# Whole-tile loads of the experts' weights, values transposed one projection later, and the last rows' norm in two halves

## The chip, the core and the metric

The kernel runs as one program on one core of one Trainium2 chip. The core has a matrix engine (PE, with PEld for the loads of its stationary operand), a vector engine (DVE), an activation engine (ACT), GpSimd (POOL), a sync engine (SP) that here only issues transfers, and 16 DMA engines shared by all queues. The metric is the device time of one execution in microseconds (us); a run's time is given, and the median over runs.

## The reference, cut to what matters

The computation takes 512 tokens of width 1024 through two residual blocks. Three of its parts are touched by the change.

```python
# first block: mixture of experts, 64 experts of width 512, two for each token
def expert_block(args):
    xb, e = args
    hid = jax.nn.silu(xb @ w_gate[e]) * (xb @ w_up[e])
    return hid @ w_down[e]
# second block: bidirectional gated linear attention, 4 heads with values of 128
...
contrib = jnp.einsum('bhncd,bhnce->bhnde', k * jnp.exp(b_last - b), v)
...
o = rmsnorm_2(o, norm_g) * jax.nn.silu(r.reshape(B, T, GLA_HEADS, GLA_DV))
# second block: squared-relu MLP of width 4096, then the last norm
h = h + sqrelu_mlp(h, ln_ff_g[l], w_ff1[l], w_ff2[l])
return rmsnorm_2(h, ln_final_g)
```

All is float32. The weights of the experts are 3 x 64 matrices of 2 MiB, together 402 MB, and each is read once.

## The kernel before

**Order in time.** The first block's mixer and the routing run until about 410 us, the experts until about 1360 us, the second block's attention, linear attention and MLP until the end. A framework schedules the instructions of each engine within a stretch by itself; the experts' matmuls are pinned in program order (`mm`, L985), and SP issues its loads in one queue.

**Experts.** `experts` (L963) walks over 32 pairs. For one pair it multiplies the gathered tokens with the gate matrices of both experts (L1059), then with the up matrices, combines the pair before into the residual `H` (`bring`, L1187 and L1190), transposes the hidden rows, and multiplies them with the two down matrices in two passes of 512 columns (names `y` and `tp`). A product walks over k-slices `j` and, inside, over the two experts `s`, whose halves of 64 columns run side by side on PE. So a product needs both experts' tiles from its first step on.

**Their weights.** `ring` (L113) hands out 9 buffers of 2 MiB in turn; a load into a buffer waits until PE has read what the load overwrites, region by region. `load` cuts a matrix into `n` pieces along the k-slices and issues each as one transfer of 128 rows, one row for a partition:

```python
n = 4 if e0 < 12 else 2
one = lambda shape, w, e: [self.ring(shape, w[e + s], 8 if e == 2 and w is wg else n) for s in range(2)]
```

`e0` is the first expert of a pair. A row is therefore 4 KB long for the first twelve experts and 8 KB after that. SP holds at most 8 loads in flight: the ninth waits for the first to land. The last pair comes in interleaved halves and quarters through `pair` (L131), the down matrices of the last two pairs after all gate and up matrices.

**Linear attention.** `values(n)` (L1591) projects one head's values (24 matmuls into `pj`, three for each k-slice: L178 and L179 read `wH`, L180 reads `wL`, the two parts into which `wsplit` cuts the weights on ACT and DVE), scales them on DVE into `x`, and transposes `x` on PE in four pieces (L1597) into `vt`. `decays` fills DVE with exponentials' products, `states` (L1629) builds the running states from `vt` and `kd`, `head` (L1654) projects the gate and makes the output of a head.

**End.** `wout_tail` (L379) multiplies the last part of the MLP for four blocks `t` of 128 rows in two halves of 512 columns and adds each half to `H` (L399). `each(t)` normalizes the block's rows (`normed`, L1319: square with sum on ACT, `rsqrt_of` on one column, one product on DVE) and stores it.

Of the kernel before, what the change touches and what calls it, by code (L numbers as in the profile page):

```python
# [6 lines left out]
FT = mybir.dt.float32  # L7
# [3 lines left out]
AF = mybir.ActivationFunctionType  # L11
OP = mybir.AluOpType
# [3 lines left out]
P = 128  # L16
T = 512
D = 1024
KT = 8
NT = 4  # L20
EPS = 1e-6
# [7 lines left out]
class Net:  # L29
# [346 lines left out]

        return [[t[:, 2 * half:2 * half + 2, :] for t in tiles] for half in range(2)]

    def wout_tail(self, W, h, mix, rs, each, between=None, behind=None):  # L379

        nc = self.nc
        banks = {}

        def product(t, half):
            if half == 0:
                banks[t] = [self.psum(("pj", "tp")[t % 2]) for _ in range(2)]
            for k in range(4):
                w = W[k // 2, half]
                m = self.mm3(banks[t][half], (mix[0][:, k, t * P:(t + 1) * P], mix[1][:, k, t * P:(t + 1) * P]),
                             (w[0][:, k % 2, :], w[1][:, k % 2, :]), k == 0, k == 3)  # L390
                if behind and k == 0:
                    self.order(behind, m)

        def add(t, half):
            o = h[:, t, half * 512:half * 512 + 512]
            if rs is None:
                nc.vector.tensor_tensor(o, banks[t][half], o, OP.add)
            else:
                nc.vector.scalar_tensor_tensor(o, banks[t][half], rs[:, t:t + 1], o, op0=OP.mult, op1=OP.add)  # L399
        product(0, 0)  # L400
        product(0, 1)
        if between:
            between()
        for t in range(NT):
            add(t, 0)
            add(t, 1)
            if t + 1 < NT:
                product(t + 1, 0)
            if each and 1:
                each(t)  # L410
            if t + 1 < NT:
                product(t + 1, 1)
            if each and not 1:
                each(t)
# [548 lines left out]
    def experts(self, keep, pool, front, inner, then):  # L963
        tc, nc, i = self.tc, self.nc, self.ins
        V = nc.vector
# [3 lines left out]
        wd = i["w_down"][0].rearrange("e (p j) n -> e p j n", j=4)  # L969

        def weights(e0):
            n = 4 if e0 < 12 else 2
            one = lambda shape, w, e: [self.ring(shape, w[e + s], 8 if e == 2 and w is wg else n) for s in range(2)]
            up, dn = [P, KT, 512], [P, 4, D]
            if e0 == 60:

                late.extend((lambda: one(dn, wd, 60), lambda: self.pair(dn, (wd[62], wd[63]))))
                return [(one(up, wg, 60), one(up, wu, 60), None),
                        (self.pair(up, (wg[62], wg[63])), self.pair(up, (wu[62], wu[63])), None)]
            return [(one(up, wg, e0), one(up, wu, e0), one(dn, wd, e0))]  # L980
# [62 lines left out]
        halves = [slice(half * 512, half * 512 + 512) for half in range(2)]  # L1043
# [7 lines left out]
        for i in range(32):  # L1051
            q, pr = i // 2, i % 2
            e0 = 2 * i
# [30 lines left out]
            rs, gs, at = vals[q]  # L1084
            r, g = rs[:, pr:pr + 1], gs[:, pr:pr + 1]
# [6 lines left out]
            turn = gained(i + 1) if 0 < i < 31 else iter(())  # L1092
# [3 lines left out]
            p = self.psum("tp")  # L1096
# [72 lines left out]
            if i == 3:  # L1169
                n = self.overflow_count(keep, front.tile([P, 64], FT, name="more", tag="eq", bufs=1))  # L1170
# [390 lines left out]
    def gla(self, small, pool, wp, w_in, A, mix, w_out, gates):  # L1561
        nc, i = self.nc, self.ins
        mm = nc.tensor.matmul
        V = nc.vector
# [7 lines left out]
        for n in range(4):  # L1572
            p = self.proj(self.wsplit(wp, wqk[:, :, n * P:(n + 1) * P], P), A)
# [5 lines left out]
        for tp in range(2):  # L1579
            p = self.psum("tp")  # L1580
            for t in range(2):
                for n in range(2):
                    o = (2 * t + n) * P
                    c = (2 * tp + t) * P
# [4 lines left out]
        vt = one("vt", [P, NT, 512])  # L1589

        def values(n):  # L1591
            p = self.proj(self.wsplit(wp, wv[:, :, n * P:(n + 1) * P], P), A)
            x = tmp("x")
            V.tensor_tensor(x, p, self.rb, OP.mult)
            p = self.psum("tp")
            for c in range(NT):
                nc.tensor.transpose(p[:, c * P:(c + 1) * P], x[:, c * P:(c + 1) * P], self.ident)  # L1597
            self.copy(vt[:, :, n * P:(n + 1) * P], p.rearrange("p (c k) -> p c k", c=NT))

        def decays(pr):  # L1600

# [49 lines left out]

        rs, og = [], []

        def head(hd, qd, ki, st):  # L1654
            s = hd % 2
            p = self.proj(self.wsplit(wp, wr[:, :, hd * P:(hd + 1) * P], P), A)
            sr = tmp("sr")
            V.tensor_tensor(sr, p, self.rb, OP.mult)
            nc.scalar.activation(sr, sr, AF.Silu)
            M = []  # L1660
            for d in range(2):
                p = self.psum("sc")
                for c in range(NT):
                    cs = slice(c * P, (c + 1) * P)
                    mm(p[:, cs], ki[s][half(d), cs], qd[s][half(d), cs], start=True, stop=True)
                t = pool.tile([P, NT, P], FT, name="M", bufs=2)
                V.tensor_tensor(t, p.rearrange("p (c k) -> p c k", c=NT),
                                mask[d][:, None, :].to_broadcast([P, NT, P]), OP.mult)
                M.append(t)
            o = self.psum("y")  # L1670
            for c in range(NT):
                cs = slice(c * P, (c + 1) * P)
                todo = [(vt[:, c, hd * P:(hd + 1) * P], M[d][:, c, :], cs) for d in range(2)]
                for n in (2 * c, 2 * c + 1):
                    ns = half(n)
                    todo.append((st[:, n, :], qd[s][:, ns], ns))
                for x, (a, b, to) in enumerate(todo):
                    last = mm(o[:, to], a, b, start=x == 0, stop=x == len(todo) - 1)  # L1678
            sq = tmp("sq")
            nc.scalar.activation(sq, o, AF.Square)  # L1680
            if s == 0:
                og.append(pool.tile([P, 2, T], FT, name="og", tag="kt" if hd else "la0", bufs=1))
            V.tensor_tensor(og[hd // 2][:, s, :], o, sr, OP.mult)
            p = self.psum("tp")
            for c in range(NT):
                mm(p[:, c:c + 1], sq[:, c * P:(c + 1) * P], self.ones[:, :1], start=True, stop=True)
            rs.append(self.rsqrt(small, p[:, :NT], NT, 1.0 / 128))
            return last
# [12 lines left out]


        *qk0, kd0 = decays(0)
        values(0)
        values(1)
        st = {0: states(0, qk0[2], kd0)}
        values(2)
        st[1] = states(1, qk0[2], kd0)
        *qk1, kd1 = decays(1)
        values(3)  # L1710
        wr = self.ring([P, KT, 512], w_in[:, :, 2560:3072])
        wt = self.ring([P, 4, D], w_out[:, 4:8, :])
        head(0, *qk0[:2], st[0])
        st[2] = states(2, qk1[2], kd1)
        last = head(1, *qk0[:2], st[1])
        normed(0, last)
# [9 lines left out]
    def ffn(self, pool, wp, A, r3):  # L1726
        nc, i, h = self.nc, self.ins, self.H
        V = nc.vector
        w1 = i["w_ff1_2"][0].rearrange("(k p) n -> p k n", p=P)
        w2 = i["w_ff2_2"][0].rearrange("(k p) n -> p k n", p=P)  # L1730
        for q in range(4):
            mixes = []
            for b in range(2):
                w = self.ring([P, KT, 512], w1[:, :, (2 * q + b) * 512:(2 * q + b + 1) * 512])
                m = self.mixtile(pool)
                mixes.append(m)
                for j in range(4):
                    p = self.proj(self.wsplit(wp, w[:, :, j * P:(j + 1) * P], P), A, P, 2 if q + b == 0 and j < 2 else 1)
                    r = pool.tile([P, T], FT, name="r", bufs=2)
                    nc.scalar.activation(r, p, AF.Relu)  # L1740
                    s = pool.tile([P, T], FT, name="s", bufs=2)
                    V.scalar_tensor_tensor(s, p, 0.0, r, op0=OP.max, op1=OP.mult)
                    self.split(m[0][:, j, :], m[1][:, j, :], s)
            w = [self.ring([P, 4, D], w2[:, 8 * q + 4 * b:8 * q + 4 * b + 4, :]) for b in range(2)]
            srcs = lambda half, s: w[s // 2][:, 2 * (s % 2):2 * (s % 2) + 2, half * 512:half * 512 + 512]
            if q < 3:
                self.wout(wp, h, srcs, mixes, r3)
            else:
                self.wout(wp, h, srcs, mixes[:1], r3)
                g = self.row(pool, "ln_final_g_2")  # L1750
                out = self.out[0].rearrange("(c p) d -> p c d", p=P)
                self.wout_tail(self.tail_weights(wp, self.halves(self.mixtile(pool)), w[1]), h, mixes[1], r3,
                               lambda c: nc.sync.dma_start(out[:, c, :], self.normed(pool, h[:, c, :], g)))


class Begin:
# [111 lines left out]
```

## Time and profile before

| | us |
|---|---|
| three runs | 2029.66, 2025.50, 2029.56 |
| median | 2029.56 |
| profiled execution | 2025.04 |
| its span, first to last instruction | 2023.3 |
| PE busy in it | 1928.0 (95%) |
| DVE busy | 946.3 (47%) |
| ACT busy | 534.7 (26%) |
| q1, the loads that SP issues | 483.63 MB, 60% of 16 DMA engines |

Times are read within the span. A row of a timeline gives its start, how long it or its merged group took, the engine, the line of the kernel, the operation with its output and inputs, a count, and in brackets how long the engine stood idle ahead of it and what ended that. A busy PE is not PE at its peak: matmuls are pipelined and a group's time is that of the group.

### The profile page before, as it was taken

The numbers are of one execution on the slowest core, as the hardware profiler recorded it, in microseconds if no ns is written. First come the engines' busy times: TensorE is split into PE (matmuls) and PEld (weight loads), VectorE is DVE, ScalarE is ACT, GpSimd is POOL, SyncE is SP. The second block draws the span as 40 slices with busy tenths as digits, with TensorE's granted clock in tenths as the row PEclk, the third lists the DMA queues.
The fourth block names the chain that finished last, engine by engine and source line by source line (L and its number), as shares of the span: only waits on it lengthen the run. The fifth ranks groups of instructions, "written<-read, shape, count | busy, mean of one in ns | idle before, by whom it ended". The sixth has DMA issues, their size and how long they took to land. (4 is left out here: it accounts for less than half of the span.)

```text
span 2023.3 us, 24002 instructions
## 1 busy us (share of the span) xinstructions
PE 1928.0 (95%) x9535; PEld 1209.0 (60%) x9535; DVE 946.3 (47%) x1891; ACT 534.7 (26%) x900; POOL 191.2 (9%) x245
## 2 busy tenths in 40 slices
PE   7999999999999999999999899999999999999998
PEld 5788777734444344343343344348767788888886
DVE  6764667733543243253243243235656654444355
ACT  5773445311010000000000000024443343223232
POOL 5211333110000000000000000002201010000000
PEclk9999999999999999999999999999999999999999
DMA  7312022799999999999999999984212112313211
GB/s 204 115 43 83 32 81 97 268 343 415 415 425 425 424 424 424 424 424 425 424 423 423 421 424 422 422 335 87 92 42 84 43 52 84 125 48 119 103 64 42
DMA packets 114777, 494.24 MB, mean 244 GB/s; under 512 B 16492, under 2 KB 23091, under 8 KB 74984
## 3 DMA queue, kind: packets, MB, share of 16 engines
q1 hardware_dynamic: 107720, 483.63, 60.0%
q0 software_dynamic: 6352, 6.96, 1.5%
q10 hardware_dynamic: 592, 2.10, 0.3%
q8 instruction: 76, 1.25, 0.3%
q14 instruction: 37, 0.30, 0.0%
HBM read 500.68 MB, written 6.15 MB: 250 GB/s over the span
## 5 line engine op out<-in xcount | busy, mean ns | idle before, releaser
L986 PE MATMUL pj<-w,xg 128*64 128x512 f32 x1696 | 467.8, 603 | 47.1 <-DMA w<-in_w_up 45.8
L986 PEld LDWEIGHTS pj<-w,xg 128*64 128x64 f32 x1696 | 152.5, 139 | 334.0 <-issue 257.5
L159 DVE TENSOR_TENSOR wL<-w,wH 128x1024 fp32r<-128x1024 f32 x135 | 167.4, 1241 | 201.1 <-ACT wH L158 198.4
L158 ACT CAST wH<-w 128x1024 fp32r<-128x1024 f32 x136 | 142.3, 1048 | 336.3 <-PE pj L179 163.9
L1091 DVE SCALAR_TENSOR_TENSOR hid<-pj,slots,hid 128x512 f32<-128x512 f32 x30 | 22.5, 751 | 426.8 <-PE pj L986 412.4
L1190 DVE TENSOR_TENSOR H<-sc,H 128x512 f32<-128x512 f32 x248 | 156.5, 683 | 6.2 <-PE sc L1187 3.5
L986 PE MATMUL pj<-w16x,xg 128*64 128x512 f32 x352 | 153.7, 619 | 0.9 <-DMA w16x<-in_w_gate 0.9
L1187 PE MATMUL sc<-yH,ST 128*128 128x512 f32 x256 | 112.7, 440 | 0.6 <-DVE H L1190 0.6
L843 POOL DMA_INDIRECT rows<-hd,tok x31 | 31.7, 1022 | 817.1 <-DVE gates L837 574.3
L1100 ACT COPY hT<-tp 128x512 f32<-128x512 f32 x32 | 18.8, 587 | 339.9 <-PE tp L1098 339.9
L180 PE MATMUL pj<-n3H,wL 128*128 128x512 f32 (+1 forms) x272 | 103.6, 381 | 0.8 <-DVE wL L159 0.8
L178 PE MATMUL pj<-n3H,wH 128*128 128x512 f32 (+1 forms) x272 | 103.6, 381 | 0.0
L179 PE MATMUL pj<-n3L,wH 128*128 128x512 f32 (+1 forms) x272 | 103.5, 380 | 0.0
L178 PE MATMUL pj<-A,wH 128*128 128x512 f32 x240 | 97.3, 405 | 4.0 <-ACT wH L158 2.8
L1187 PE MATMUL sc<-yL,ST 128*128 128x512 f32 x252 | 99.9, 396 | 0.0
L178 PE MATMUL sc<-wH,mixH 128*128 128x512 f32 x252 | 98.5, 391 | 0.4 <-ACT wH L158 0.4
L179 PE MATMUL sc<-wL,mixH 128*128 128x512 f32 x252 | 98.4, 390 | 0.1
L180 PE MATMUL sc<-wH,mixL 128*128 128x512 f32 x252 | 98.2, 390 | 0.0
L179 PE MATMUL pj<-A,wH 128*128 128x512 f32 x240 | 96.8, 403 | 0.0
L180 PE MATMUL pj<-A,wL 128*128 128x512 f32 x240 | 96.2, 401 | 0.5 <-DVE wL L159 0.5
L986 PE MATMUL y<-w,hT 128*64 128x512 f32 x336 | 78.0, 599 | 0.7 <-DMA w<-in_w_down 0.7
L986 PE MATMUL tp<-w,hT 128*64 128x512 f32 x336 | 76.5, 592 | 0.0
(586 smaller groups left out, 3279.6 us busy)
## 6 DMA issues: line engine op xcount, KB each, us to landing
w<-in_w_up SPq DMA_DIRECT2D x88, 1024.0 KB, 20.8
w<-in_w_gate SPq DMA_DIRECT2D x84, 1024.0 KB, 19.6
w<-in_w_down SPq DMA_DIRECT2D x70, 1024.0 KB, 19.6
w16x<-in_w_down SPq DMA_DIRECT2D x32, 1024.0 KB, 20.2
w<-in_w_ff SPq DMA_DIRECT2D x16, 2048.0 KB, 7.8
w<-in_w_in SPq DMA_DIRECT2D x12, 2048.0 KB, 10.4
w<-in_w_up SPq DMA_DIRECT2D x40, 512.0 KB, 9.9
w16x<-in_w_gate SPq DMA_DIRECT2D x20, 1024.0 KB, 19.8
```

The lines of the kernel that those rows point to most:

```text
L158: a = nc.scalar.copy(H, src)
L159: b = (engine or nc.vector).tensor_tensor(L, src, H.bitcast(FT), OP.subtract)
L178: m = mm(out, lH, rH, start=first, stop=False)
L179: mm(out, lH, rL, start=False, stop=False)
L180: mm(out, lL, rH, start=False, stop=last)
L843: self.nc.gpsimd.indirect_dma_start(out=rows, out_offset=None, in_=self.hd[:, :], in_offset=bass.IndirectOffsetOnAxis(ap=tok, axis=0), bou ...
L986: return self.pin(nc.tensor.matmul(*a, **k))
L1091: V.scalar_tensor_tensor(hid, pu, r, hid, op0=OP.mult, op1=OP.mult)
L1100: nc.scalar.copy(hT.rearrange("p j s -> p (j s)"), p)
L1187: m = nc.tensor.matmul(p, ST[:n, t * P:(t + 1) * P], y[:n], start=k == 0, stop=k == len(mms) - 1)
L1190: nc.vector.tensor_tensor(h[:, t, hs], p, h[:, t, hs], OP.add)
```

## The change

Three edits. The pieces of a weight matrix are fewer: two up to expert 7, one from expert 8 on, the very first gate matrices of expert 2 and 3 and the last pair as before. `values` returns its transposes as a function, and the callers run it after the next projection, the last one inside the first `head`. In `wout_tail` a hook runs after the last block's first half is added: it squares that half and multiplies it with the gain; the rest of the norm then covers the second half alone on DVE, with the first half scaled on ACT and stored through ACT's queue.

```diff
--- before.py
+++ after.py
@@ -376,7 +376,7 @@
 
         return [[t[:, 2 * half:2 * half + 2, :] for t in tiles] for half in range(2)]
 
-    def wout_tail(self, W, h, mix, rs, each, between=None, behind=None):
+    def wout_tail(self, W, h, mix, rs, each, between=None, behind=None, half_done=None):
 
         nc = self.nc
         banks = {}
@@ -403,6 +403,8 @@
             between()
         for t in range(NT):
             add(t, 0)
+            if half_done and t == NT - 1:
+                half_done()
             add(t, 1)
             if t + 1 < NT:
                 product(t + 1, 0)
@@ -969,7 +971,7 @@
         wd = i["w_down"][0].rearrange("e (p j) n -> e p j n", j=4)
 
         def weights(e0):
-            n = 4 if e0 < 12 else 2
+            n = 2 if e0 < 8 else 1
             one = lambda shape, w, e: [self.ring(shape, w[e + s], 8 if e == 2 and w is wg else n) for s in range(2)]
             up, dn = [P, KT, 512], [P, 4, D]
             if e0 == 60:
@@ -1592,10 +1594,13 @@
             p = self.proj(self.wsplit(wp, wv[:, :, n * P:(n + 1) * P], P), A)
             x = tmp("x")
             V.tensor_tensor(x, p, self.rb, OP.mult)
-            p = self.psum("tp")
-            for c in range(NT):
-                nc.tensor.transpose(p[:, c * P:(c + 1) * P], x[:, c * P:(c + 1) * P], self.ident)
-            self.copy(vt[:, :, n * P:(n + 1) * P], p.rearrange("p (c k) -> p c k", c=NT))
+
+            def turn():
+                p = self.psum("tp")
+                for c in range(NT):
+                    nc.tensor.transpose(p[:, c * P:(c + 1) * P], x[:, c * P:(c + 1) * P], self.ident)
+                self.copy(vt[:, :, n * P:(n + 1) * P], p.rearrange("p (c k) -> p c k", c=NT))
+            return turn
 
         def decays(pr):
 
@@ -1651,9 +1656,11 @@
 
         rs, og = [], []
 
-        def head(hd, qd, ki, st):
+        def head(hd, qd, ki, st, between=None):
             s = hd % 2
             p = self.proj(self.wsplit(wp, wr[:, :, hd * P:(hd + 1) * P], P), A)
+            if between:
+                between()
             sr = tmp("sr")
             V.tensor_tensor(sr, p, self.rb, OP.mult)
             nc.scalar.activation(sr, sr, AF.Silu)
@@ -1701,16 +1708,19 @@
 
 
         *qk0, kd0 = decays(0)
-        values(0)
-        values(1)
+        a = values(0)
+        b = values(1)
+        a()
         st = {0: states(0, qk0[2], kd0)}
-        values(2)
+        a = values(2)
+        b()
         st[1] = states(1, qk0[2], kd0)
         *qk1, kd1 = decays(1)
-        values(3)
+        a()
+        a = values(3)
         wr = self.ring([P, KT, 512], w_in[:, :, 2560:3072])
         wt = self.ring([P, 4, D], w_out[:, 4:8, :])
-        head(0, *qk0[:2], st[0])
+        head(0, *qk0[:2], st[0], a)
         st[2] = states(2, qk1[2], kd1)
         last = head(1, *qk0[:2], st[1])
         normed(0, last)
@@ -1749,8 +1759,30 @@
                 self.wout(wp, h, srcs, mixes[:1], r3)
                 g = self.row(pool, "ln_final_g_2")
                 out = self.out[0].rearrange("(c p) d -> p c d", p=P)
-                self.wout_tail(self.tail_weights(wp, self.halves(self.mixtile(pool)), w[1]), h, mixes[1], r3,
-                               lambda c: nc.sync.dma_start(out[:, c, :], self.normed(pool, h[:, c, :], g)))
+                halves = [slice(0, 512), slice(512, D)]
+                x = pool.tile([P, D], FT, name="nl", bufs=1)
+                ss = pool.tile([P, 2], FT, name="nl2", bufs=1)
+
+                def half_done():
+
+                    nc.scalar.activation(x[:, halves[1]], h[:, 3, halves[0]], AF.Square, accum_out=ss[:, 0:1])
+                    V.tensor_tensor(x[:, halves[0]], h[:, 3, halves[0]], g[:, halves[0]], OP.mult)
+                    V.tensor_scalar(ss[:, 0:1], ss[:, 0:1], 1.0 / D, EPS, op0=OP.mult, op1=OP.add)
+
+                def tile_done(c):
+                    if c < 3:
+                        nc.sync.dma_start(out[:, c, :], self.normed(pool, h[:, c, :], g))
+                        return
+                    nc.scalar.activation(x[:, halves[1]], h[:, 3, halves[1]], AF.Square, accum_out=ss[:, 1:2])
+                    v = pool.tile([P, 1], FT, name="rv", bufs=2)
+                    V.scalar_tensor_tensor(v, ss[:, 1:2], 1.0 / D, ss[:, 0:1], op0=OP.mult, op1=OP.add)
+                    r = self.rsqrt_of(pool, v, 1)
+                    V.scalar_tensor_tensor(x[:, halves[1]], h[:, 3, halves[1]], r, g[:, halves[1]], op0=OP.mult, op1=OP.mult)
+                    nc.sync.dma_start(out[:, 3, halves[1]], x[:, halves[1]])
+                    nc.scalar.activation(x[:, halves[0]], x[:, halves[0]], AF.Copy, scale=r)
+                    nc.scalar.dma_start(out[:, 3, halves[0]], x[:, halves[0]])
+                self.wout_tail(self.tail_weights(wp, self.halves(self.mixtile(pool)), w[1]), h, mixes[1], r3, tile_done,
+                               half_done=half_done)
 
 
 class Begin:
```

How it moves instructions, first on SP, where the loads of a pair in the middle of the experts stand (`w` and `w16x` are buffers of the ring; 128x2048 is half a matrix). Before:

```order
L149 DMA w_3921<-in_w_down 128x1024 x4
L149 DMA w_3930<-in_w_down 128x1024 x4
L1172 TENSOR_LOAD nover
L1172 ISA x2
L149 DMA w_3736<-in_w_gate 128x2048 x2
L149 DMA w_3741<-in_w_gate 128x2048 x2
L149 DMA w_3746<-in_w_up 128x2048 x2
L149 DMA w_3751<-in_w_up 128x2048 x2
```

and now:

```order
L149 DMA w_3909<-in_w_down 128x4096
L149 DMA w_3918<-in_w_down 128x4096
L1174 TENSOR_LOAD nover
L1174 ISA x2
L149 DMA w_3736<-in_w_gate 128x4096
L149 DMA w_3739<-in_w_gate 128x4096
L149 DMA w_3742<-in_w_up 128x4096
L149 DMA w_3745<-in_w_up 128x4096
```

Each matrix is one load in place of two, in the same order and the same buffers; the read of the overflow count stands between the same pairs.

On PE, the transposes of the first head's values (`tp<-ident,x`). Before, after the first matmul of the second head's projection:

```order
L178 MATMUL pj<-n2H,wH 128x512
L179 MATMUL pj<-n2L,wH 128x512
L180 MATMUL pj<-n2H,wL 128x512
L178 MATMUL pj<-n2H,wH 128x512
L1597 MATMUL tp<-ident,x 128x128 x4
L179 MATMUL pj<-n2L,wH 128x512
L180 MATMUL pj<-n2H,wL 128x512
```

and now, behind that projection's 24 matmuls, ahead of the third head's:

```order
L178 MATMUL pj<-n2H,wH 128x512
L179 MATMUL pj<-n2L,wH 128x512
L180 MATMUL pj<-n2H,wL 128x512
L1601 MATMUL tp<-ident,x 128x128 x4
L178 MATMUL pj<-n2H,wH 128x512
L179 MATMUL pj<-n2L,wH 128x512
L180 MATMUL pj<-n2H,wL 128x512
L178 MATMUL pj<-n2H,wH 128x512
```

The four transposes have moved by one projection; the second head's projection now follows the first without a break.

On DVE, the end of the program: the first half of the last block's addition, the norm of the third block (`nx`) and the second half of the addition. Before:

```order
L399 SCALAR_TENSOR_TENSOR H<-tp,r_11097,H 128x512
L241 TENSOR_SCALAR ra<-ra 128x1
L243 TENSOR_TENSOR rr<-rr,ra 128x1
L1326 SCALAR_TENSOR_TENSOR nx<-H,rr,row_ln_final_g_13182 128x1024
L399 SCALAR_TENSOR_TENSOR H<-tp,r_11097,H 128x512
L229 TENSOR_SCALAR rv<-ns 128x1
```

and now:

```order
L399 SCALAR_TENSOR_TENSOR H<-tp,r_10867,H 128x512
L241 TENSOR_SCALAR ra<-ra 128x1
L1769 TENSOR_TENSOR nl<-H,row_ln_final_g_12952 128x512
L243 TENSOR_TENSOR rr<-rr,ra 128x1
L1770 TENSOR_SCALAR nl_12955<-nl_12955 128x1
L1328 SCALAR_TENSOR_TENSOR nx<-H,rr,row_ln_final_g_12952 128x1024
L399 SCALAR_TENSOR_TENSOR H<-tp,r_10867,H 128x512
L1778 SCALAR_TENSOR_TENSOR rv<-nl_12955 128x1
```

A product of 512 columns and a step on one column stand between the two halves of the last addition, beside what was there.

## Rows read from the trace of the kernel before

**Rows 1.** page's forty slices: DMA's busy share in tenths, then GB/s

```profile
DMA  7312022799999999999999999984212112313211
...
GB/s 204 115 43 83 32 81 97 268 343 415 415 425 425 424 424 424 424 424 425 424 423 423 421 424 422 422 335 87 92 42 84 43 52 84 125 48 119 103 64 42
```

**Rows 2.** stretches: us, busy PE, PEld, DVE, ACT, POOL, clock, DMA, GB/s

```profile
600.00:700.00 100.00, 95.00 (x428) 38.70 (x424) 32.80 (x64) 9.55 (x15) 2.23 (x3) 0.98 1.01 424
...
1000.00:1100.00 100.00, 91.62 (x420) 38.02 (x416) 34.17 (x74) 8.64 (x13) 4.04 (x4) 0.98 1.01 423
...
1700.00:1800.00 100.00, 100.00 (x436) 81.45 (x435) 40.64 (x46) 30.17 (x39) 0.00 (x0) 1.00 0.28 101
```

**Rows 3.** PE's timeline, one pair: start, us, instruction, [wait ahead, releaser]

```profile
761.40 7.08 PE L986 MATMUL pj<-w,xg 128*64 128x512 f32 x30 [2.20 <-DMA w<-in_w_up]
...
792.21 7.08 PE L986 MATMUL pj<-w,xg 128*64 128x512 f32 x30 [2.65 <-DMA w<-in_w_up]
```

**Rows 4.** waits, experts: us in total, times, longest; PE, then SP

```profile
PE pj L986 <- DMA w<-in_w_up: 45.8, 22, 3.4
...
SPq L149 <- DMA w<-in_w_up: 156.8, 72, 3.7
...
SPq L149 <- PE sc L1187: 8.9, 34, 0.4
```

**Rows 5.** DMA totals, us 460:545, 600:1300, 461:474, 566:579

```profile
DMA packets 9892, 35.27 MB, mean 415 GB/s; under 512 B 1293, under 2 KB 1293, under 8 KB 9888
...
DMA packets 43727, 296.44 MB, mean 423 GB/s; under 512 B 7213, under 2 KB 7213, under 8 KB 7925
...
DMA packets 1501, 5.47 MB, mean 421 GB/s; under 512 B 165, under 2 KB 165, under 8 KB 1501
...
DMA packets 762, 5.56 MB, mean 428 GB/s; under 512 B 83, under 2 KB 83, under 8 KB 83
```

**Rows 6.** SP's timeline at the experts' start

```profile
417.19 0.38 SPq L149 DMA_DIRECT2D w<-in_w_down  x1
...
438.50 2.90 SPq L149 DMA_DIRECT2D w16x<-in_w_gate  x4
```

**Rows 7.** PE's timeline at the experts' end

```profile
1307.97 7.08 PE L986 MATMUL pj<-w,xg 128*64 128x512 f32 x30 [2.17 <-DMA w<-in_w_up]
...
1336.23 1.07 PE L986 MATMUL y<-w,hT 128*64 128x512 f32 x2
...
1339.90 1.50 PE L986 MATMUL y<-w,hT 128*64 128x512 f32 x5 [0.49 <-DMA w<-in_w_down]
...
1341.24 4.02 PE L986 MATMUL tp<-w,hT 128*64 128x512 f32 x15
...
1349.50 7.09 PE L986 MATMUL pj<-w,hT 128*64 128x512 f32 x32
```

**Rows 8.** linear attention: PE's timeline, then DVE's

```profile
1547.67 0.63 PE L1597 MATMUL tp<-ident,x 128*128 128x128 f32 x4 [2.32 <-DVE x L1594]
...
1576.70 1.11 PE L1597 MATMUL tp<-ident,x 128*128 128x128 f32 x4 [2.42 <-DVE x L1594]
...
1547.43 1.22 DVE L159 TENSOR_TENSOR wL<-w,wH 128x1024 fp32r<-128x1024 f32 x1
...
1576.57 1.22 DVE L159 TENSOR_TENSOR wL<-w,wH 128x1024 fp32r<-128x1024 f32 x1
```

**Rows 9.** the end: DVE's and ACT's timeline, then the stores

```profile
2013.12 1.28 DVE L1326 SCALAR_TENSOR_TENSOR nx<-H,rr,row_ln_final_g 128x1024 f32<-128x1024 f32 x1
...
2014.62 0.75 DVE L399 SCALAR_TENSOR_TENSOR H<-tp,r,H 128x512 f32<-128x512 f32 x1 [0.21 <-PE tp L180]
...
2015.46 1.06 ACT L1324 ACTIVATE nx<-H 128x1024 f32<-128x1024 f32 x1 [3.86 <-DVE H L399]
...
out<-nx SPq DMA_DIRECT2D x4, 512.0 KB, 2.6
```

**Rows 10.** the page's queues: packets, MB, share of 16 engines

```profile
q8 instruction: 76, 1.25, 0.3%
```

## The prediction

> **What bounds the kernel now.** I read the page's forty slices first [rows 1]. From about 405 to 1335 us, while the experts run, the DMA line stands at 9 and the rate at 415 to 425 GB/s; outside it the rate is far lower and PE is the busy engine. The table by stretch [rows 2] says the same: the 16 DMA engines are busy for the whole of each stretch (the share is 1.01), while PE has 5 to 8 us idle in each 100; between 1700 and 1800 it is the other way round. So inside the experts the weights' arrival sets the pace. The steady pair of experts shows it [rows 3]: PE starts the up product at 761.40 after a wait of 2.20 for DMA, runs combine, down and the next gate product without a stop, and waits 2.65 again at the next up product at 792.21, 30.8 us later. These waits are 45.8 us over 22 pairs [rows 4]. The sync engine (SP), which issues the loads, waits mostly for earlier loads to land, hardly for PE [rows 4]; so the queue in front of the DMA engines is always full, and a buffer that comes free a little later costs nothing there.
>
> **Term 1: the experts' weights.** A tile is 2 MiB, 16 KB in each of 128 partitions. Before, it came as 4 loads of 4 KB rows for experts 0 to 11 and as 2 loads of 8 KB rows after that. Now it is 2 loads up to expert 7 and one load of 16 KB rows from expert 8 on; the last pair (62, 63) is unchanged. What row length is worth is in the trace [rows 5]: with 4 KB rows 35.27 MB in 85 us, 414.9 GB/s or 5.054 us per tile; with 8 KB rows 296.44 MB in 700 us, 423.5 GB/s or 4.952 us per tile. An engine moves 32 rows of a tile in the one case and 16 in the other, so the 16 rows less are worth 0.102 us: 6.4 ns a row. In two shorter stretches without the gathers of tokens (5.47 and 5.56 MB in 13 us) it is 4.984 against 4.903 us, 5.0 ns a row. No row of weights of 16 KB is in the trace. I carry the straight line on: 8 rows less in a tile are 51 ns (40 ns by the shorter stretches). The bounds are 0, if a longer row is cut or no cheaper, and 102 ns, if all of the cost by row went.
> The Trainium skill, "DMA: Bandwidth & Descriptors", section "Why small descriptors are slow (HBM only)", gives a fixed cost of about 3 cycles of an engine's internal bus for each packet; with the 850 MHz that its section "Where 436 GB/s comes from" uses, that is, as an estimate from the page, 3.5 ns a row, and the tiles below would bring 4.2 us in place of 7.5. The trace shows more, 5.0 to 6.4 ns, and I go by the trace.
> Tiles: experts 12 to 59 have 144, and 4 more (gate and up of 60 and 61) stand ahead of the last wait: 148 x 0.051 = 7.5 us. Experts 8 to 11 go from 4 KB to 16 KB: 12 x 0.153 = 1.8 us. Of the first 8 experts about 7 tiles come while the queue is already full: 7 x 0.102 = 0.7 us.
> Against this stand two costs of coarser pieces. At the start [rows 6] the loads wait for PE to free the first buffers: the queue restarts at 417 as the first gate product frees quarters, and at 438.50 as the second pass of the down product does. Halves come free 1.7 us later at the first place and 0.9 us at the second; between them four tiles move 0.1 us faster each. I take 0.5 us, bounds 0 and 1.7. At the end [rows 7] PE starts the up product of experts 60 and 61 at 1307.97, when the first half of the second tile is there, and runs 28.3 us without a wait to the down product at 1336.23; there it waits for halves of their down tiles, the last of which comes at 1339.90, and it is done at 1345.26 (1341.24 and 4.02), 5.4 us behind that landing. With whole tiles the up product starts half a tile (2.4 us) later relative to the DMA stream, and PE comes to the down product 1.2 us before its second tile has landed (six tiles at 4.9 are 29.5, PE needs 28.3); it then has all 32 matmuls left, 7.1 us as the last down product takes from 1349.50 [rows 7], in place of 5.4: 1.7 us lost, and I take 1.8. That last product starts behind PE and not behind DMA, so all of this passes on.
> Inside the steady stretch the later start of each product costs nothing: the pair's work is 30.8 less 2.65, some 28.1 us, and the DMA's period, now about 30, still leaves the wait at the up product.
> Sum of term 1: -7.5 - 1.8 - 0.7 + 0.5 + 1.8 = -7.7 us. Low end of the gain: with nothing from rows over 8 KB the 148 tiles bring 0 and the twelve 1.2 (4 to 8 KB), which makes -1.2 - 0.7 + 0.5 + 1.8 = +0.4. High end: 148 x 0.102 + 12 x 0.204 + 0.7 - 2.3 = 15.9 us gained.
>
> **Term 2: values turned behind the next projection.** PE stands 2.32 us at 1547.67 and 2.42 us at 1576.70 before the four transposes of x, both times until DVE has made x [rows 8]. The transposes move behind 24 matmuls, and the diff alone says that 4.7 us go. But the next projection's third matmul reads wL, and DVE makes wL directly behind x: 1.22 us from 1547.43, 1.22 us from 1576.57 [rows 8]. The order of DVE at these places is unchanged, x and then wL, behind the decays' work. In the trace of before PE has done the transposes at 1548.3 and 1577.8, and wL is there at 1548.65 and 1577.79: that third matmul goes when wL comes, and it can't go sooner now. The wait takes wL's name, one matmul of 0.23 is saved and four transposes (0.4 to 0.6) come later: about 0.2 lost at each. At the third projection the transposes and the states' 16 matmuls stood ahead of it and covered its wL; now fewer do, up to 1.1 us, while the states run in pairs on both halves of the array and save as much. I take +0.2 us in all; bounds -4.7 (both waits go) and +2.
>
> **Term 3: the last rows' norm in two halves.** The tail behind PE's last matmul is in [rows 9]: addition 0.75, square over 1024 columns 1.06, small steps, a product as long as the 1.28 of the third row block, and 2.6 us from issue to landing of 512 KB. Now square and product run over 512 columns. DVE's addition of 512 is 0.75, so the product gives back 0.53; the square by the same ratio is 0.62 and gives back 0.44; the other half is scaled on ACT beside DVE. But DVE's queue gets a product of 512 (0.75) and a small step (some 0.15, as an estimate) ahead of the 1.28 of the third row block, and the last addition stands behind that. The 1.28 ended at 2014.40 and PE was ready 0.21 later, at 2014.6, so 0.2 of the 0.9 is covered and 0.7 comes on the path. The two stores move the same bytes together. -1.0 + 0.7 = -0.3 us; bounds -1.3 (the delay does not show and the landing is shorter) and +0.5.
>
> **Sum.** -7.7 + 0.2 - 0.3 = -7.8 us. The profiled execution took 2025.04 us (span 2023.3), and the sum makes it 2017.2. The three runs shown are 2025.5, 2029.56 and 2029.66, so the profiled one lies 4.5 below their median; I forecast the median: 2029.56 - 7.8 = 2021.8 us.
>
> **The rivals.** (a) Both waits of PE go in the linear attention, because DVE gets to wL sooner than I read: another 4.9 us, 2016.9. For it: the waits name x and not wL. Against it: wL's rows. (b) A 16 KB row is cut into pieces of 8 KB or costs as much: term 1 is +0.4, the sum +0.3, 2029.9. For it: no weight row above 8 KB is in the trace; against it: the steps seen so far follow the cost by row. (c) Slower: 16 KB packets cost more by byte. The only ones in the trace are those of queue q8, 76 packets of 1.25 MB in 0.3% of 16 engines' span [rows 10]: 97 us, 1.28 us each, where two of 8 KB take 0.62. Against it: these go elsewhere and share an engine with the weights. Place: 148 tiles x 8 rows, so each ns above 0.612 us a row costs 1.18 us; the whole excess would be 790 us, and 2% more by byte (12 ns) 15 us, which gives 2029.56 - 7.8 + 15 = 2037. It decides from 7 ns on, where the gain is used up. (d) The diff doing nothing to the loads is excluded by SP's order, which shows the whole tiles.
>
> **How the numbers follow.** 0.62 for the forecast, by itself 2016.5 to 2026.5 (40 ns to 80 ns a tile and the bounds of the small terms); 0.12 for (a), 0.18 for (b), 0.08 for (c). A change under 0.2%, 4.1 us, can't be told from none, as the runs shown lie that far apart. Faster by more: 0.84 of the forecast's 0.62 (the term must stay above half its size) and all of (a), 0.64. Within: the rest of the forecast and most of (b), 0.26. Slower: (c) and a little of (b), 0.10. The range goes from 2014 (a with more by row) to 2029 (a part of b).
>
> **What would show it.** Term 1: the rate between 600 and 1300 rises from 423 to about 428 GB/s with the share still at 1.01, the wait at the up product stays, a wait of 1.2 us stands at the down product of experts 60 and 61, and the last down product starts some 7.7 us sooner than 1349.50. A rate of 423 is (b), a lower one (c). Term 2: in place of 2.32 and 2.42 on x, waits of 3 us on wL at the third matmul; a stretch shorter by 4 us would make (a) right. Term 3: the last addition waits no longer for PE (0.21 now) and starts some 0.7 us later behind its last matmul.

## The result

The changed kernel took 2009.43 us (median of four runs, 2006.88 to 2010.76) against 2028.28 for the kernel before on the same chip: a ratio of 0.9903, with an interval of 0.989 to 0.9916. In two later comparisons, each beside the kernel before, it was 0.9895 (0.9878 to 0.9911) and 0.9905 (0.9881 to 0.9928). That is 18.9 us faster by the medians (the ratio, as in all runs below, is not that of the medians; it makes 19.7); 7.8 were forecast (2021.8 us against 2029.56), and the range ended at 2014. The sign was right, the size was not.

Where the two traces part (starts on PE, us; lengths of the stretches between them):

| stretch | before | after | shorter by |
|---|---|---|---|
| start to the first transposes of the experts' hidden rows (430.85; 435.60) | 430.85 | 435.60 | -4.75 |
| from there to the last down product (1349.50; 1345.32) | 918.65 | 909.72 | 8.9 |
| from there to attention's last output rows (1491.11; 1485.84) | 141.61 | 140.52 | 1.1 |
| from there to the second head's output (1600.59; 1586.89) | 109.48 | 101.05 | 8.4 |
| from there to the end of the span (2023.3; 2009.1) | 422.71 | 422.21 | 0.5 |

The first line is no work of the change: the experts are reached anywhere between 430.7 and 435.6 us in the traces below, whichever edit is in them. The third is a fall of PE's clock that only the trace of before has there (0.78 of full speed from 1482 to 1486, 0.79 in the next four). The second line is term 1, the fourth term 2, which should have been -0.2, the last term 3. The fourth line ends where PE begins the output of the second of the four heads; all four heads' values have been turned by then.

The experts first, the table by stretch of the changed kernel (columns as in [rows 2]), which answers to [rows 5]:

```profile
460.00:545.00 85.00, 85.00 (x411) 37.91 (x408) 36.42 (x75) 8.54 (x13) 1.98 (x2) 1.00 1.01 428
600.00:1300.00 700.00, 660.20 (x3007) 288.35 (x3008) 249.33 (x512) 62.32 (x94) 24.27 (x24) 0.98 1.01 428
```

The rate went from 415 and 423 to 428 GB/s, with the engines as busy as before (1.01). At the experts' end PE's timeline answers to [rows 7]:

```profile
1304.04 8.78 PE L988 MATMUL pj<-w,xg 128*64 128x512 f32 x30 [1.96 <-DMA w<-in_w_up]
...
1334.00 3.65 PE L988 MATMUL y<-w,hT 128*64 128x512 f32 x16
...
1345.32 7.09 PE L988 MATMUL pj<-w,hT 128*64 128x512 f32 x32
```

The wait at the up product is there, the forecast loss at the down product is not: in this execution the 30 matmuls of the up product took 8.78 in place of 7.08 while the granted clock (the column behind POOL) had fallen, and PE came 1.7 us later:

```profile
1304.00:1308.00 4.00, 3.96 (x12) 1.24 (x14) 0.00 (x0) 0.00 (x0) 0.00 (x0) 0.58 0.99 383
```

In the linear attention both waits of [rows 8] are gone, and none on `wL` stands in their place; the one new wait of PE in the stretch is 0.39 us for `vt`, ahead of the second head's states. PE's timeline at the first of them:

```profile
1544.34 0.39 PE L180 MATMUL pj<-n2H,wL 128*128 128x512 f32 x1
1544.58 0.60 PE L1601 MATMUL tp<-ident,x 128*128 128x128 f32 x4
1544.93 0.48 PE L178 MATMUL pj<-n2H,wH 128*128 128x512 f32 x1
1545.24 0.39 PE L179 MATMUL pj<-n2L,wH 128*128 128x512 f32 x1
1545.47 0.40 PE L180 MATMUL pj<-n2H,wL 128*128 128x512 f32 x1
```

The transposes start 0.24 after the matmul ahead of them, and the next matmul on `wL` follows 0.9 later, without a wait.

At the end, DVE's timeline and then ACT's answer to [rows 9]:

```profile
1999.20 0.69 DVE L1769 TENSOR_TENSOR nl<-H,row_ln_final_g 128x512 f32<-128x512 f32 x1
...
2000.04 1.28 DVE L1328 SCALAR_TENSOR_TENSOR nx<-H,rr,row_ln_final_g 128x1024 f32<-128x1024 f32 x1
2001.24 0.74 DVE L399 SCALAR_TENSOR_TENSOR H<-tp,r,H 128x512 f32<-128x512 f32 x1
...
2004.23 0.75 DVE L1780 SCALAR_TENSOR_TENSOR nl<-H,rr,row_ln_final_g 128x512 f32<-128x512 f32 x1
...
2002.08 0.63 ACT L1776 ACTIVATE nl<-H 128x512 f32<-128x512 f32 x1 [2.15 <-DVE H L399]
```

### The profile page after: what moved, and what is told of

It is laid out like the page before. It is cut to its first block, busy times and chain, and to the rows that moved or that the text cites. A ratio compares the mean times of both kernels' runs of the same rounds, so it can differ in the third digit from the quotient of the medians.

```text
span 2009.1 us, 23641 instructions
## 1 busy us (share of the span) xinstructions
PE 1926.2 (96%) x9535; PEld 1214.9 (60%) x9535; DVE 947.6 (47%) x1893; ACT 535.7 (27%) x903; POOL 192.2 (10%) x245
```

## The experiments

### Each edit alone

Three kernels, each the kernel before with one of the three edits of the diff and nothing else. The weights:

> The experts' weights in whole tiles alone, on the kernel before. By the forecast's term 1: 7.7 us faster (0.38%), about 2020.6 against 2028.3, with 428 GB/s between 600 and 1300 us and the end of the experts some 8 to 9 us sooner. By the rival that the whole difference of 18.9 us comes from the weights: about 2009.5. In between, by the stage's length in the two traces (918.7 us from the first expert's transposes to the last down product before, 909.7 after): 9.0 us faster.

Measured: 2019.19 us, ratio 0.9956 (0.9941 to 0.997): 8.9 us faster by the ratio, 6 to 12 by the interval; 428 GB/s, and 909.85 us from the first expert's transposes to the last down product. The forecast's 7.7 and the stage's 9.0 both lie within; the rival that all comes from the weights falls. The turned values:

> The turned values behind the next projection alone, on the kernel before. By the forecast's term 2 (the wait goes over to wL): 0.2 us slower, no difference. By the theory that wL of the next projection was made long before, so that nothing is late in the wait's place: the two waits of 2.32 and 2.42 us go, 4.7 us faster; with the lower clock behind the second wait (0.80 and 0.77 over 8 us, 1.7 us) 6.4 us faster; the stretch in the two traces is 8.4 us shorter. So 4.7 to 8.4 us faster, 2020 to 2023.6.

Measured: 2019.72 us, ratio 0.9956 (0.994 to 0.9971), 8.9 us faster. Term 2 of the forecast is refuted by this run; the theory that nothing is late in the wait's place holds: 8.9 is a little above the 4.7 to 8.4 it expected, which the interval (6 to 12) covers. The norm:

> The last rows' norm in two halves alone, on the kernel before. By the forecast's term 3: 0.3 us faster; the last addition about 0.7 us later behind PE's last matmul, what follows it 1.0 us shorter. By the rival that the delay doesn't show: 1.3 us faster; by the other end 0.5 us slower. Within 0.2% in every case.

Measured: 2029.02 us, ratio 1.0004 (0.9994 to 1.0015): no difference, as in every case expected. The product of the three ratios is 0.9916, at the edge of the whole change's interval. So the parts add up as far as intervals of 2 to 3 us to either side can tell; a further gain of a few us that the edits have only together is not excluded.

The linear attention (from the last rows of attention's output to the second head's output) in three traces, before, the weights alone, and changed:

```profile
1491.11:1600.59 109.48, 103.41 (x584) 83.38 (x584) 67.94 (x116) 37.20 (x50) 11.84 (x10) 0.98 0.16 58
```

```profile
1483.49:1594.62 111.13, 105.08 (x584) 84.48 (x584) 67.81 (x116) 37.20 (x50) 11.82 (x10) 0.97 0.16 57
```

```profile
1485.84:1586.89 101.05, 99.33 (x584) 80.95 (x585) 66.81 (x116) 37.00 (x50) 11.86 (x10) 1.00 0.18 63
```

The work is the same in the first two, and the second is 1.65 us longer: there the granted clock falls behind both waits, in the trace of before only behind the second. So the stretch is 107.8 without a fall, and 6.8 us of the gain are there without the clock. PE's idle time (the length less its busy time) goes from 6.07 to 1.72, its busy time at full clock by another 2.4.

### One wait of the two

`values` returns its transposes as in the change; the callers are cut to:

```diff
-        values(0)
-        values(1)
+        a = values(0)
+        b = values(1)
+        a()
+        b()
         st = {0: states(0, qk0[2], kd0)}
-        values(2)
+        values(2)()
...
-        values(3)
+        values(3)()
```

> On the kernel before: the first head's transposes alone move behind the second projection; the second head's follow at once and the other two stay. By the theory that nothing is late in the wait's place: the wait of 2.32 us goes and the first head's states run in pairs (half of the 2.0 us that the four stretches gain, one of two places), so the linear attention is 3.3 us shorter than before at the same number of clock falls; the wait of 2.42 us at the last head's x stays. By the forecast (the wait takes wL's name): 0.2 us longer, with a wait of about 2.3 us on wL in it.

Measured in one execution (2025.35 us): the stretch is 106.26 us (1494.61 to 1600.87), 3.2 shorter than before at the same one fall; no wait on `wL`. PE at the last head's x, where nothing was moved:

```profile
1576.82 1.03 PE L1599 MATMUL tp<-ident,x 128*128 128x128 f32 x4 [2.42 <-DVE x L1594]
```

2.32 of the 3.2 are the wait. The other 0.9 lies in the first head's `states`, which take 1.11 us from first to last in place of 2.70 with 0.66 of transposes in the middle. Before, PE's timeline has its matmuls for one half of the array, then the second head's transposes, then those for the other half:

```profile
1552.88 1.08 PE L1637 MATMUL y<-vt,kd 64*64 64x128 f32 x14
1553.90 0.66 PE L1597 MATMUL tp<-ident,x 128*128 128x128 f32 x4
1554.48 0.76 PE L1637 MATMUL tp<-vt,kd 64*64 64x128 f32 x10
```

and in the changed kernel, as in this one, the two halves start 0.01 us apart and run beside each other:

```profile
1546.27 0.33 PE L1642 MATMUL tp<-vt,kd 64*64 64x128 f32 x2
1546.28 0.33 PE L1642 MATMUL y<-vt,kd 64*64 64x128 f32 x2
```

In the changed kernel the second head's states change in the same way (2.69 to 1.11), so about 2 of the 8.4 us come from there.

### x ahead of the decays' work

```diff
-        *qk0, kd0 = decays(0)
         values(0)
+        *qk0, kd0 = decays(0)
...
-        *qk1, kd1 = decays(1)
         values(3)
+        *qk1, kd1 = decays(1)
```

> On the kernel before: the first head's values are projected ahead of the first decays, the last head's ahead of the second decays, transposes where they were, directly behind their projection. It takes away what made x late by the new theory: DVE's work for the decays, which stood ahead of x. If that queue made the waits of 2.32 and 2.42, x is there within about 1 us, the waits go and the kernel is 4 to 8 us faster, unless the decays, which now come later, make the states wait for kd by about as much (then no difference). If the wait stood for wL, as the forecast said, x still has wL behind it and nothing changes by more than 0.5 us.

Measured: 2025.49 us, ratio 0.9986 (0.9975 to 0.9997), 2.8 us faster by the ratio, less than the 4 to 8. DVE's timeline shows why:

```profile
1542.79 0.69 DVE L1594 TENSOR_TENSOR x<-pj,rb 128x512 f32<-128x512 f32 x1 [3.96 <-PE pj L180]
1543.56 1.23 DVE L159 TENSOR_TENSOR wL<-w,wH 128x1024 fp32r<-128x1024 f32 x1
1545.47 0.69 DVE L1614 TENSOR_TENSOR kd<-kd,kt 128x512 f32<-128x512 f32 x1 [0.68 <-ACT kd L1613]
...
1554.53 0.69 DVE L1594 TENSOR_TENSOR x<-pj,rb 128x512 f32<-128x512 f32 x1
1555.13 1.22 DVE L159 TENSOR_TENSOR wL<-w,wH 128x1024 fp32r<-128x1024 f32 x1
```

The first x now waits for PE, as it should; the decays' work behind it fills DVE until the second head's x, and PE waits 2.01 us for that one. Two waits of 2.3 and 2.4 became one of 2.0, and PE waits 0.91 for `M` at the first head's output, which it did not before. The stretch by this trace:

```profile
1492.52:1599.29 106.77, 102.41 (x585) 82.44 (x585) 69.64 (x116) 37.21 (x50) 13.19 (x10) 1.00 0.17 60
```

That is 1.0 less than the 107.8 of before without a fall of the clock, and none fell here, behind the wait of 2.01 either. Whichever x stands behind the decays is late, and `wL` follows x at once in both places without anyone waiting for it.

### PE kept at work while it waits

```diff
             p = self.psum("tp")
+            for _ in range(13 * (n in (0, 3))):
+                mm(p, A[0][:, 0, :P], A[0][:, 0, :], start=True, stop=True)
             for c in range(NT):
```

> On the kernel before: 13 matmuls of 512 columns, whose results are thrown away, stand on PE directly ahead of the transposes of the first and of the last head's x, so that PE works (13 x 0.233 = 3.0 us) while it would wait; the transposes now stand ahead of the four matmuls of the next projection that were ahead of them, so each place loses 4 x 0.233 = 0.9 us. If the lower clock behind the two places (two of three in the traces of before and of the weights alone, 1.7 us each) comes from PE's standing still, the granted clock stays at 1.00 from 1545 to 1600 us, while it may still fall behind the untouched wait of 2.6 us ahead of it; the linear attention then takes 107.8 (no fall) + 1.9 = 109.7 us. If the fall has another cause, it is there at one place or both and the stretch takes 111.3 to 113.

Measured in one execution (2031.06 us): the stretch is 109.86 us (109.7 expected). The table by stretch at the untouched wait of 2.61 us, then behind the two that were filled:

```profile
1488.00:1492.00 4.00, 3.85 (x18) 2.37 (x18) 2.36 (x8) 1.17 (x2) 0.00 (x0) 0.63 0.00 0
1492.00:1496.00 4.00, 4.00 (x32) 3.15 (x30) 0.69 (x1) 0.00 (x0) 0.79 (x4) 0.52 0.00 0
...
1552.00:1556.00 4.00, 3.81 (x20) 2.86 (x19) 2.19 (x3) 0.59 (x1) 0.00 (x0) 1.00 0.00 0
...
1582.00:1586.00 4.00, 3.58 (x19) 2.67 (x18) 2.81 (x4) 0.00 (x0) 0.00 (x0) 1.00 0.00 0
```

The clock falls behind the one and not behind the others. In the traces with those two waits left open it fell behind 8 of 9 (both in the weights alone, the norm alone and the 4 KB rows below; the second of two before; the one left open where only the other was moved); the expectation's "two of three" is three of four by the traces it names. So in this one execution the fall went when PE was kept at work, and the waits cost more than they show: 1.7 us in most of these traces. It is not a rule without exceptions, as the wait of 2.01 above shows.

### Row length or number of loads

In the first kernel all experts but the last pair come in quarters (`n = 4`). In the second, on the changed kernel, a matrix from expert 8 on is still one load, with two rows of 8 KB for a partition (the view `"(h p r) n -> p h (r n)"` with `h=2`).

> On the kernel before: every expert's matrix but the last pair's in four loads of 4 KB rows. By the forecast's price of 6.4 ns a row: 148 tiles get 16 rows an engine more, 148 x 0.102 = 15.1 us slower (ratio 1.0074), the rate between 600 and 1300 us 415 GB/s; less by up to 1.8 us where finer pieces let PE start earlier at the end. If row length were not what counts (rival (b)): no difference.

Measured: 2042.41 us, ratio 1.0084 (1.0066 to 1.0101), 17 us slower by the ratio (15.3 by the medians); 412 GB/s between 600 and 1300 us:

```profile
DMA packets 81827, 288.68 MB, mean 412 GB/s; under 512 B 11447, under 2 KB 11447, under 8 KB 81788
```

That is 5.085 us for a tile of 2 MiB in place of 4.952, so 0.133 where the forecast's price made 0.102. Rows and loads change together here; the next kernel parts them.

> The changed kernel with each matrix from expert 8 to 61 still in one load, but in two rows of 8 KB for a partition, from the two halves of the matrix; the products therefore meet the weights' rows in another order than the tokens' columns, so only the time means something. If the row's length makes the gain: 8 KB rows again, 423 GB/s between 600 and 1300 us, 7 to 8 us slower than the changed kernel (ratio to before 0.994). If it is the number of loads, of which at most 8 are in flight: 428 GB/s and the changed kernel's time (0.990).

Measured: 2016.14 us, ratio 0.9944 (0.9921 to 0.9966), with the changed kernel beside it at 0.9905:

> The changed kernel beside the one above on the same chip: 0.990 of before, 428 GB/s.

The transfers between 600 and 1300 us before, with one load of two 8 KB rows, and changed:

```profile
DMA packets 43727, 296.44 MB, mean 423 GB/s; under 512 B 7213, under 2 KB 7213, under 8 KB 7925
```

```profile
DMA packets 41602, 297.17 MB, mean 425 GB/s; under 512 B 4997, under 2 KB 4997, under 8 KB 5709
```

```profile
DMA packets 24026, 299.92 MB, mean 428 GB/s; under 512 B 5026, under 2 KB 5026, under 8 KB 5738
```

The means of the second and the changed kernel are 7.0 us apart (interval 2 to 12), as expected if the row's length makes the gain. By the megabytes moved in the 700 us a tile takes 4.952, 4.940 and 4.895 us. One load less brings 0.012 us, 8 rows less an engine 0.045: 5.7 ns a row. So row length is four fifths of the gain in rate. The load's own price shows as well: 2216 packets under 512 B are gone with about 141 loads, some 16 a load. In this kernel a partition's two rows lie in the two halves of the matrix, in the kernel before next to each other; what that does by itself no run shows.

A third kernel cut the whole tiles by partitions instead (two loads of 64 partitions, rows of 16 KB):

> The changed kernel with the whole tiles of expert 8 and up in two loads of 64 partitions each, rows 16 KB long as in one load, loads as many as before the change. If the row's length makes the rate: 428 GB/s and the time of the changed kernel (ratio to before 0.990). If it is the number of loads, of which at most 8 are in flight: 423 GB/s and about 8 us slower than the changed kernel (ratio 0.994). If 64 partitions are served more slowly than 128: a lower rate than 423 and slower than that.

Measured: 2564.78 us, from 2395.3 to 2640.99; the fastest of the four executions is 368 us above the median of the kernel before on the same chip. It tells nothing about row length, since the third expectation came true, far beyond what I meant by it. The trace is that of the slowest execution:

```profile
600.00:1300.00 700.00, 443.70 (x1550) 166.67 (x1552) 129.88 (x264) 31.78 (x48) 12.21 (x12) 0.79 1.01 223
```

### A version that beats both

```diff
-            if j == 3:
-                zT = self.low_ranks(small, pool, wp, wz, A)
             attend(j, *now)
+            if j == 3:
+                zT = self.low_ranks(small, pool, wp, wz, A)
```

> The changed kernel once more, to have it beside the next one on the same chip: a ratio of 0.990 to before. By the sum of its parts (0.9956 x 0.9956 x 1.0004 as measured one by one) 0.9916; by a gain that the parts don't have alone, 0.990 or lower.

> The changed kernel with one more move of the same kind: the low-rank projection of the gates is written behind the last pair of attention heads instead of ahead of it. PE then does the scores first and the projection while DVE and ACT make the softmax, and DVE has no work for the gates ahead of the scores' maxima. If the wait of 2.61 us for S at 1479.80 has the same cause as those in the linear attention, it goes, and with it the lower clock that follows it in four of seven traces: 2.6 us faster than the changed kernel, 3.5 with the clock. If S is then late for another reason (its chain of ACT's eight exponentials, about 4 us), a part of the wait stays: 1 us. If the gates' rows become late instead: no gain.

(The fall had been there in three of six traces by then, not in four of seven.) Measured: the changed kernel 2007.78 us, ratio 0.9895; this one 2003.07 us, ratio 0.988 (0.9862 to 0.9897). The means of four runs each are 3.7 us apart, with an interval of 0.6 to 6.8. PE's wait for `S`, the attention's weights behind the softmax, in the changed kernel, and here:

```profile
1477.75 1.15 PE L1455 MATMUL tp<-ident,S 128*128 128x128 f32 x8 [2.61 <-DVE S L1451]
```

```profile
1472.35 1.15 PE L1455 MATMUL tp<-ident,S 128*128 128x128 f32 x8 [1.02 <-DVE S L1451]
```

From the last down product to the second head's output the two traces, neither with a fall of the clock there, take 241.60 and 238.25 us. PE's wait for S is 1.02, with one of 0.55 ahead of it, in place of 2.61, and the wait of 0.67 for `mixH` (attention's output) behind it is gone, as are two of under 0.2: 2.1 us of the 3.4. The rest is matmuls that follow each other more closely (1.2 us less of PE's busy time). So a part of the wait stays, as in the second case, and the gain of 3.4 lies above the first case's 2.6 without the clock. The move gives PE other work and takes work off DVE at the same time; which of the two shortened the wait, no run parts.

## Why the prediction was wrong

**Term 2 was the step that failed**: "the next projection's third matmul reads wL, and DVE makes wL directly behind x". The `wL` made behind x is not that of the next projection but of the one after it. The weights are split one projection ahead, and names without buffer numbers look alike. The trace of before had it, in PE's and DVE's timelines:

```profile
1544.71 0.40 PE L180 MATMUL pj<-n2H,wL 128*128 128x512 f32 x1
...
1548.36 0.40 PE L180 MATMUL pj<-n2H,wL 128*128 128x512 f32 x1
...
1535.59 1.22 DVE L159 TENSOR_TENSOR wL<-w,wH 128x1024 fp32r<-128x1024 f32 x1 [0.16 <-ACT wH L158]
```

The matmul at 1544.71 belongs to the second projection already (24 matmuls at 0.233 from 1538.57 end at 1544.2) and reads a `wL` ahead of PE's wait; the one at 1548.36 starts 0.29 before the `wL` of [rows 8] is finished at 1548.65. The forecast wrote that this matmul "goes when wL comes"; its start was earlier than that. The `wL` that both read is the one of 1535.59, there 8 us before. So nothing is late in the wait's place: term 2 was given +0.2, with bounds of -4.7 and +2, and measured -8.9 by the ratio (-8.4 between the two traces). Rival (a) was the true case, at a chance of 0.12; its reason, that DVE gets to `wL` sooner, holds only in that the `wL` which counts was an earlier one.

Rival (a) was too small as well: 4.9 us for the two waits and term 2's 0.2 where the edit alone gave 8.9. Its price left out the states' matmuls that pair up (2.0; the forecast counted them only to set off a loss) and the clock (1.7 for each fall). The trace of before had a stretch of four microseconds at 0.57 behind the second wait:

```profile
1576.00:1580.00 4.00, 3.30 (x10) 2.80 (x11) 2.47 (x3) 0.00 (x0) 0.00 (x0) 0.57 0.02 4
```

The four transposes of [rows 8] at 1576.70 took 1.11 in place of 0.63, a sign that was copied and not read.

**Term 1** was right: -7.7 forecast, -8.9 measured (6 to 12). The rate came out at 428 as written. The price of a row, 6.4 ns (5.0 by the short stretches), is 5.7 with the load's own 12 ns beside it, which together make 57 ns a tile in place of 51: 148 x 0.057 = 8.4 us in place of 7.5. The forecast had no term for the load, but its line carried the load's price along, since from 4 KB to 8 KB rows the loads had halved too. The Trainium skill's 3.5 ns a row, as an estimate from "DMA: Bandwidth & Descriptors", section "Why small descriptors are slow (HBM only)", is below the 5.7 of these runs. The end cost came as forecast where the up product ran at full clock, as in the best version:

```profile
1300.22 7.08 PE L988 MATMUL pj<-w,xg 128*64 128x512 f32 x30 [1.93 <-DMA w<-in_w_up]
...
1328.49 4.32 PE L988 MATMUL y<-w,hT 128*64 128x512 f32 x15
...
1332.65 4.02 PE L988 MATMUL tp<-w,hT 128*64 128x512 f32 x15
```

PE needs 28.27 us to the down product (28.3 forecast), and the product takes 8.18 (1328.49 to 1336.67) where the changed kernel's, which comes behind the landing, takes 7.09 (1334.00 to 1341.09). The profile names no wait there, since one expert's first matmuls run alone, but 1.1 us goes there where a wait of 1.2 was forecast.

**Term 3**: -0.3 forecast, within 0.2% of nothing as said. The traces give -0.5: from PE's last matmul to the end of the span 8.7 before, 8.2 after. The delay of the last addition is 0.29 (0.33 behind PE's end in place of 0.04), not 0.7: the product at 1999.20 runs in part while DVE would have waited between the small steps, so the third block's product starts 0.59 later behind the first half's addition and not 0.9, and 0.3 of that is covered by what was a wait for PE.

**The difference of the medians** (18.9) is the sum of 8.9, 8.9 and 0.5, within their intervals.

## What to carry to other kernels

Before a wait is said to pass to another tile, find which buffer the next reader reads and when it was made: the first read of that tile ahead of the wait, or a start before the supposed producer's end, settles it. In the second block here PE's waits of 2.3 to 2.6 us cost their length and, in 15 of 21 cases, a stretch at the lower clock behind it (1.7 us), so count both, and look at the granted clock of the few microseconds behind each wait that a change removes. Where the transfers were the bound here, the longest row a tile allows was worth having even from 8 to 16 KB, but not at the price of fewer partitions in a load.

## What the runs showed that I had not expected

- Loads of 64 partitions moved 223 GB/s in the trace of the slowest of four executions, where loads of 128 move 428, with the engines' busy share at 1.01 in both; no run here says why.
- Each load brings some 16 packets of under 512 B and costs about 0.012 us of a full queue (one trace against the kernel before).
- The same wait of 2.61 us for `S` was followed by a fall of the clock in 7 of 12 traces and in 5 not; what decides is open. The experts' part of the trace of before is like it: from 600 to 1310 us PE waits 16 times for 2.2 to 3.4 us, and the clock falls 7 times, each time within 1.3 us of the end of one of these waits.
